# A hybrid encoder layer: the second copies of the dilated heads' high halves are loaded, and w_out's low parts are made on GpSimd in two steps

## The chip, the cores and the metric

One core of one Trainium2 chip runs the kernel. The time is the device time of one execution in microseconds (us). Engines are named as in the profile: PE is TensorE's matmuls, DVE is VectorE, ACT is ScalarE, POOL is GpSimd, SP is SyncE, which here issues the DMAs.

## The reference

```python
h = layer_norm(x, g_emb, b_emb)                     # (1, 2048, 1024)
proj = h @ w_in                                     # a_q a_k a_v a_g c_q c_kv b_kr b_g m_q m_g
y_a = dilated_attention(rope(a_q), rope(a_k), a_v)  # 16 heads of 64; (window, dilation) = (128,1), (512,4), (2048,16),
                                                    # each 64 neighbours a side; the three merged by their softmax sums
q = rms_norm(c_q) @ w_uq;  kv = rms_norm(c_kv) @ w_ukv
y_b = softmax((q_nope k_nope + q_rope k_rope) * 96**-0.5) @ v   # latent attention (MLA): 8 heads, all 2048 keys
y_m = softmax(m_q mk * 128**-0.5) @ mv                          # 4 heads on 256 memory tokens
y = concat(rms_norm(y_g) * silu(gate_g) for g in (a, b, m))     # (1, 2048, 2048)
out = layer_norm(alpha * h + y @ w_out, g_post, b_post)
```

All of it is float32. The kernel gets near that with 16-bit matmuls by splitting a number in a high part (its 16-bit rounding) and a low part (what the rounding left out): a product then takes three matmuls, high x high, high x low and low x high.

## The kernel before, in words

The work runs in four stages on the one core: layer norm, projections, gates and memory attention (0 to some 1370 us of the trace); the sixteen dilated heads (to 1745); the eight latent heads (to 2442); and the output stage, which transposes y and multiplies it by w_out (to the end). Instructions of an engine run in the order in which they were written; a wait of one holds all that stand behind it on its engine.

**A dilated head** is ten units: four of the first pattern, four of the second (u = 4 to 7), two of the third. A unit computes 128 x 1024 scores in PSUM (L1819 adds a mask, L1828 multiplies keys by queries), `probabilities` makes `pf` = exp(scores) on ACT (L1500), `ph`, its 16-bit rounding (on DVE, L1507 or L1513, or on ACT, L1505 or L1511), and `pl` = pf - ph (L1508 or L1514, on DVE or POOL); in the units 0 and 4 to 7 one half of `pf` goes through two selects on POOL (L1769) instead of a mask. `engines` (L1773) holds the choice: `pl` is on POOL in the units 1, 5, 6 and 8. `attend` multiplies by the values (L1521 to L1523), and `Out.add` copies a filled PSUM tile to the stage tile `so` (L1800, on DVE for the patterns 1 and 2). `Pipeline.push` writes a unit's multiplication by values three units behind its scores.

The scores of a head take two products over 128 and 65 rows: keys `ks` with queries `qs` (high parts in rows 0 to 63, low parts in 64 to 127), and `kk` with `q1`, which hold the other pairings: rows 0 to 63 of `kk` are the high keys again, rows 0 to 63 of `q1` are the lower half of `qs`. All of these tiles are named hq in the profile. `load_head` (L1289) loads `ks`, `qs` and a row of `q1` for the next head, into the other of two sets of tiles, when a head's first unit is written; SP issues it. `repeat_parts` (L1297) then makes the repeated rows, in four pieces of 512 columns each, the last of `kk` 768: of `kk` on ACT (L1302), of `q1` on DVE (L1304). `PIECES` (L1752) writes two of these copies behind each of the units 4 to 7 of the head before. For head 0 all eight stand at the end of the first stage.

**A latent head** is 4 blocks of 512 queries (n) by 8 units (k2) of 256 keys; a chunk below is one n of one head. Units are written in pairs by `push_two`. A unit multiplies keys by queries (L1654 to L1656), and two products of the running maximum of a later head stand beside it (L1602, into the PSUM tile `ps_x`), each reduced by DVE (`lmc`, L1608; `lmx`, L1612, ends sixteen of them). `pf`, `ph` and `pl` are as above; `lo_eng` (L1723) puts every third `pl` on POOL, the others on DVE. L1679 to L1681 multiply by the values; at a chunk's end L1686 and L1687 divide.

**w_out's 16 chunks of 128 rows** are scaled by a column `fw` and split in `woh` and `wol` in the latent heads 0 to 4 and the second chunk of head 5, one for each n of 1 to 3. In latent_units (L1696 to L1703) `load_raw` loads a chunk into the one float32 tile `wo_raw` at k2 = 0, `high` (L1988, ACT) makes `woh` at k2 = 4 and `low` (L1993, DVE) makes `wol` = raw x fw - woh at k2 = 6. At that k2 `busy` is set to 2: the next two `pl` go to POOL, and the count of three starts anew.

**The output stage** prepares its first tiles beside the last latent heads: `two` (L2032, POOL) and `three` (L2036, DVE) add the three patterns' results, `scale_a` and `scale_b` (L2045, L2048, POOL) multiply by gates.

Of the kernel before, what the change touches and what calls it, by code (L numbers as in the profile page):

```python
# [16 lines left out]
ALU = mybir.AluOpType  # L17
# [5 lines left out]
NT, NCH, NQ = S // P, D // P, S // 512  # L23
AH, AE = 16, 64
BH = 8
# [10 lines left out]
WRAP = 256  # L36
# [26 lines left out]
def tile_layer(ctx: ExitStack, tc: tile.TileContext, x, mem, pos, invf, sgn, g_embT, b_embT, g_emb, b_emb, w_in,  # L63
               g_cqT, g_ckvT, w_uq, w_ukv, w_mkv, g_outT, w_out, g_post, b_post, out):
    nc = tc.nc
# [34 lines left out]
    q_r = scratch("q_r", [AH, 2 * AE, S], F16)  # L100
    k_n = scratch("k_n", [AH, 2 * AE, S + WRAP], F16)
# [217 lines left out]
    sets, msets, vsets = [None, None], [None, None], [None, None]  # L319
    with ExitStack() as p1:  # L320
# [969 lines left out]
        def load_head(h):  # L1290
            ks, qs, q1, kk = sets[h % 2]
            nc.sync.dma_start(out=ks, in_=k_n[h])
            nc.sync.dma_start(out=qs, in_=q_r[h])
            nc.sync.dma_start(out=q1[64:65, :].rearrange("p (r k j) -> p r k j", r=16, k=8),
                              in_=AP(mneg, h * S, [[0, 1], [16, 16], [256, 8], [1, 16]]))

        def repeat_parts(h, i):  # L1297

            ks, qs, q1, kk = sets[h % 2]
            c = slice(512 * (i % 4), 512 * (i % 4) + 512 + (WRAP if i == 3 else 0))  # L1300
            if i < 4:
                nc.scalar.copy(kk[0:64, c], ks[0:64, c])  # L1302
            else:
                nc.vector.tensor_copy(q1[0:64, c], qs[64:128, c])  # L1304


        with tc.tile_pool(name="up", bufs=2, side="right", reuse_waits="tile") as up:
            gains = up.tile([P, 3], F32, bufs=1, name="gains")
# [175 lines left out]
        for n in (3, 0, 1, 2):  # L1484
            for g, w in zip((14, 15), two):
                gate_chunk(g, w, n, step)
            if n == 3:
                hpools[3].close()
                vs0 = early.enter_context(ExitStack())
                vsets[0] = value_set(vs0.enter_context(tc.tile_pool(name="vs0", bufs=1, side="right", reuse_waits="tile")))  # L1490
                vals0 = load_values(0)
                ones_rows(sets[0])
                for i in range(8):
                    repeat_parts(0, i)

    W2 = 1024
    def probabilities(pool, ps, scale, lo_engine, hi_engine=None, bufs=(4, 6), pair=None, select=None, bias=shift_t):
# [131 lines left out]
    def latent_units(h):  # L1629
# [62 lines left out]
        for n in range(NQ):  # L1692
            for k2 in range(8):
                if (n, k2) == (0, 0 if h else 2):
                    begin()
                if n and len(wol) < NT:  # L1696
                    if k2 == 0:
                        raws.append(load_raw(la, len(woh), 1))
                    if k2 == 4:
                        high(raws[0])  # L1700
                    busy[0] = 2 * (k2 == 6) or busy[0]
                    if k2 == 6:
                        low(raws.pop())  # L1703
                yield unit(n, k2)

    def all_heads():
# [11 lines left out]
                            ended.append((heads[h], m))  # L1718
                        yield

    lo_turn, busy = [0], [0]

    def lo_eng():  # L1723
        lo_turn[0] += 1
        if busy[0]:
            busy[0] -= 1
            lo_turn[0] = 0
            return nc.gpsimd
        return nc.gpsimd if lo_turn[0] % 3 == 0 else nc.vector

    raws, planned = [], {}
    ended = []
# [16 lines left out]
    for g, i in ((2, 0), (1, 1), (0, 1), (1, 0), (0, 0)):  # L1749
        stage[g][i] = da.tile([P, 16, 130], F32, bufs=1, name=f"so{g}_{i}")  # L1750

    LO, HI, PIECES = (1, 5, 6, 8), (0, 2, 3, 4, 8), {4: (0, 4), 5: (1, 5), 6: (2, 6), 7: (3, 7)}  # L1752


    BARE = {4: (1,), 5: (1,), 6: (1,), 7: (1,), 0: (1,)}
# [154 lines left out]
    def all_units():  # L1910
        vals = vals0
        for h in range(AH):
            if h % 2 and h + 1 < AH:
                following = load_values(h // 2 + 1)
            units = head_units(h // 2, h % 2, vals)
            if h == 0:
                ones_rows(sets[1])
            if h + 1 < AH:
                load_head(h + 1)
                for i, unit in enumerate(units):  # L1920
                    yield unit
                    for piece in PIECES.get(i, ()):
                        repeat_parts(h + 1, piece)
                    if h + 2 == AH and i == 4:
                        vs0.close()
                if h + 2 == AH:
                    s0.close()
            else:
                lvp = late.enter_context(tc.tile_pool(name="lv", bufs=1, side="right", reuse_waits="tile"))
                lv.extend(lvp.tile([P, NT * 258], F16, name=f"lv{i}") for i in range(2))  # L1930
                msets[0] = head_set(m0.enter_context(tc.tile_pool(name="m0", bufs=1, side="right", reuse_waits="tile")), 0, F16)
                head = Head(0)
                load_lv(0)
                for i, unit in enumerate(units):
                    yield unit
                    if i in MAXU:
                        max_tile(head, MAXU.index(i))
                    if i == 8:
                        head.max_turn(0, bank("s"))
            if h % 2 and h + 1 < AH:  # L1940
                vals = following
# [25 lines left out]
    with ExitStack() as p4:  # L1967
# [7 lines left out]
        woh = []  # L1975
# [9 lines left out]
        def high(raw):  # L1985
            c = len(woh)
            woh.append(wo0.tile([P, D], F16, name=f"woh{c}"))
            nc.scalar.activation(woh[c], raw, AF.Copy, scale=fw[:, c:c + 1])  # L1988

        def low(raw):  # L1990
            c = len(wol)
            wol.append(wo0.tile([P, D], F16, name=f"wol{c}"))
            nc.vector.scalar_tensor_tensor(out=wol[c], in0=raw, scalar=fw[:, c:c + 1], in1=woh[c], op0=ALU.mult, op1=ALU.subtract)  # L1993

        y_of, gates = {}, {}

# [315 lines left out]
```

## Time and profile before

| what | value |
|---|---|
| median of 3 runs | 2823.1 us (2821.95, 2823.10, 2834.79) |
| profiled execution | 2826.99 us, span 2825.1 us |
| latent stage, 1745 to 2442 us: PE / DVE / ACT / POOL busy | 661 / 560 / 558 / 270 us of 697 |
| dilated stage, 1370 to 1745 us: PE / DVE / ACT / POOL busy | 331 / 317 / 320 / 307 us of 375 |
| data moved | 347 MB, mean 123 GB/s |

A row of a group reads: line, engine, operation, tiles out<-in, shapes and count, then busy time in us and the mean of one in ns, then the idle time of the engine just before these instructions and what ended most of it. A row of the timeline has the start (us from the span's start), the duration, and in brackets the idle time before it. A row of the view of waits: us in total, times, longest.

### The profile page before, as it was taken

What the parts mean: (1) busy time and instruction counts of PE and PEld (TensorE: products, weight loads), DVE (VectorE), ACT (ScalarE), POOL (GpSimd) and SP (SyncE); (2) the same over time, 40 slices, a digit from 0 to 9 for tenths busy, and PEclk for the clock granted to TensorE, in tenths of its full rate; (3) what the DMA queues carried; (4) which work ended last, traced back from release to release, by engine and by line L of the source; (5) the groups of instructions that cost most, each with busy time, mean ns of one, the idle gap of its engine ahead of it and who ended that gap; (6) DMA issues with size and microseconds to landing.
All of it is one profiled execution on the core that took longest, in us unless ns stands there. A gap on an engine that the chain in (4) does not pass through costs nothing.

```text
span 2825.1 us, 56944 instructions
## 1 busy us (share of the span) xinstructions
PE 2666.0 (94%) x22765; PEld 1604.6 (57%) x22765; DVE 1926.0 (68%) x4427; ACT 1612.3 (57%) x2197; POOL 970.1 (34%) x649
## 2 busy tenths in 40 slices
PE   7989999999999999989988888999999999899998
PEld 6644445545546675455677776555555656545444
DVE  7524244449994576744588879788777878577776
ACT  6645434442123565544688887788777868533332
POOL 5301013342233000211588885434444333222221
PEclk9999999999999999999999999999999999999999
DMA  5556336682224212467488785212212030256663
GB/s 168 153 170 188 94 104 164 166 194 88 82 87 149 72 42 75 131 198 211 157 183 202 215 158 119 58 31 67 62 50 59 17 78 12 74 173 187 187 190 102
DMA packets 280489, 347.32 MB, mean 123 GB/s; under 512 B 38816, under 2 KB 209056, under 8 KB 279200
## 3 DMA queue, kind: packets, MB, share of 16 engines
q1 hardware_dynamic: 280224, 343.69, 44.0%
q8 instruction: 178, 2.92, 0.4%
q14 instruction: 87, 0.71, 0.1%
HBM read 216.13 MB, written 127.45 MB: 122 GB/s over the span
## 4 chain that ended last, share of the span: by engine, by line
PE 45%; DVE 9%; issue 4%; DMA 4%; ACT 3%; POOL 2%; SPq 0%; DVEq 0%; ACTq 0%; POOLq 0%
PE ps_s L2115 10%; PE ps_mm L189 6%; PE ps_x L1602 3%; PE ps_s L1654 3%; PE ps_s L1655 3%; PE ps_s L1656 3%; PE ps_o L1680 2%; PE ps_o L1681 2%; PE ps_o L1679 2%; PE ps_x L189 2%; PE ps_s L1828 2%; DVE lmc L1608 2%; PE ps_x L2115 1%; ACT pf L1500 1%; DVE pl L1514 1%
## 5 line engine op out<-in xcount | busy, mean ns | idle before, releaser
L189 PE MATMUL ps_mm<-hT,w_h 128*128 128x512 f16 x2880 | 862.9, 382 | 6.1 <-DVE rp L669 3.1
L189 PE MATMUL ps_mm<-hT,w_l 128*128 128x512 f16 x1440 | 547.3, 381 | 0.2 <-DVE w_l L396 0.2
L1514 POOL TENSOR_TENSOR pl<-pf,ph 128x1024 f16<-128x1024 f32 x134 | 342.1, 2556 | 450.1 <-ACT ph L1511 368.0
L189 PEld LDWEIGHTS <-w_h 128*128 128x128 f16 x2880 | 271.6, 99 | 277.5 <-issue 25.4
L1608 DVE TENSOR_REDUCE lmc<-ps_x 128x1 f32<-128x512 f32 x496 | 318.3, 684 | 123.8 <-PE ps_x L1602 122.8
L1500 ACT ACTIVATE pf<-ps_s,lscale 128x1024 f32<-128x1024 f32 x256 | 285.9, 1117 | 126.2 <-PE ps_s L1656 108.9
L1511 ACT ACTIVATE ph<-ps_s,lscale 128x1024 f16<-128x1024 f32 x254 | 283.9, 1118 | 0.0
L1514 DVE TENSOR_TENSOR pl<-pf,ph 128x1024 f16<-128x1024 f32 x200 | 270.8, 1355 | 4.7 <-ACT ph L1511 1.9
L189 PEld LDWEIGHTS <-w_l 128*128 128x128 f16 x1440 | 141.4, 98 | 172.2 <-issue 3.1
L1681 PE MATMUL ps_o<-lv,pl 128*128 128x65 f16 x2032 | 211.5, 197 | 7.4 <-POOL pl L1514 7.4
L1679 PE MATMUL ps_o<-lv,ph 128*128 128x65 f16 x2032 | 212.3, 197 | 0.0
L1680 PE MATMUL ps_o<-lv,ph 128*128 128x64 f16 x2032 | 211.9, 199 | 0.0
L1500 ACT ACTIVATE pf<-ps_s,shift_t,ascale 128x1024 f32<-128x1024 f32 x160 | 191.2, 1209 | 32.3 <-PE ps_s L1828 16.7
L1679 PEld LDWEIGHTS <-ph 128*128 128x128 f16 x2032 | 194.5, 99 | 22.1 <-issue 10.7
L1654 PE MATMUL ps_s<-hq,hq 97*128 97x512 f16 x512 | 198.0, 387 | 6.7 <-ACT ph L1511 3.4
L1680 PEld LDWEIGHTS <-ph 128*128 128x128 f16 x2032 | 194.8, 100 | 16.0 <-issue 2.0
L1681 PEld LDWEIGHTS <-pl 128*128 128x128 f16 x2032 | 194.4, 102 | 7.7 <-POOL pl L1514 7.6
L1655 PE MATMUL ps_s<-hq,hq 96*128 96x512 f16 x512 | 197.2, 385 | 0.0
L1656 PE MATMUL ps_s<-hq,hq 96*128 96x512 f16 x512 | 195.4, 382 | 0.0
L966 DVE CUSTOM_DVE_ANT_0 d1j<-ps_x,wm 128x256 bf16<-128x256 f32 (+1 forms) x608 | 184.5, 364 | 2.2 <-PE ps_x L963 1.4
L1828 PE MATMUL ps_s<-hq,hq 128*128 128x256 f16 (+3 forms) x1536 | 185.2, 259 | 0.0
L1602 PE MATMUL ps_x<-hq,hq 96*128 96x512 f16 x496 | 154.7, 384 | 30.8 <-DVE lmc L1608 30.7
(416 smaller groups left out, 5874.0 us busy)
## 6 DMA issues: line engine op xcount, KB each, us to landing
w_raw<-in_w_in_dram SPq DMA_DIRECT2D x56, 512.0 KB
oa<-oa_d SPq DMA_DIRECT2D x48, 520.0 KB
v<-va_d SPq DMA_DIRECT2D x24, 1032.0 KB
oa_d<-so SPq DMA_DIRECT2D x16, 1040.0 KB
gate_d<-sg SPq DMA_DIRECT2D x64, 256.0 KB
lv<-gate_d SPq DMA_DIRECT2D x15, 1024.0 KB
hq<-k_n SPq DMA_DIRECT2D x16, 576.0 KB
oa_d<-so SPq DMA_DIRECT2D x32, 260.0 KB
```

The costliest lines, as they stand in the source:

```text
L189: nc.tensor.matmul(ps, R(a), R(b), start=(i == 0), stop=(i == n - 1))
L1500: nc.scalar.activation(pf, ps, AF.Exp, bias=bias, scale=scale)
L1511: nc.scalar.activation(ph, ps, AF.Exp, bias=bias, scale=scale)
L1514: pipe.later.append(lambda: lo_engine.tensor_tensor(out=pl, in0=pf, in1=ph, op=ALU.subtract))
L1608: nc.vector.tensor_reduce(out=self.mc[:, t % 4, n:n + 1], in_=ps, axis=AX.X, op=ALU.max)
L1654: nc.tensor.matmul(b, R(cur.kh[0:97, kc]), R(cur.qh[0:97, c]), start=True, stop=False)
L1655: nc.tensor.matmul(b, R(cur.kh[0:96, kc]), R(cur.ql[0:96, c]), start=False, stop=False)
L1656: nc.tensor.matmul(b, R(cur.kl[0:96, kc]), R(cur.qh[0:96, c]), start=False, stop=True)
L1679: nc.tensor.matmul(o, ph, v[:, 0:65], start=(k2 == 0 and j == 0 and i == 0), stop=False, skip_group_check=True)
L1680: nc.tensor.matmul(o[:, 0:64], ph, v[:, 65:129], start=False, stop=False, skip_group_check=True)
L1681: nc.tensor.matmul(o, pl, v[:, 0:65], start=False, stop=(k2 == 7 and j == 1 and i == 3), skip_group_check=True)
L2115: nc.tensor.matmul(po[a // 512][:, a % 512:a % 512 + b - a], R(y[:, kc]), R(w[:, a:b]), start=(k == 0 and i == 0), stop=(k == NT - 1 and i ...
```

## The change

1. `load_head` issues two more DMAs on SP for each head, from DRAM, for the repeated rows of `kk` and `q1`; `repeat_parts`, `PIECES` and the eight copies of head 0 are gone.
2. `low` is two instructions on POOL: `scaled` at k2 = 5 multiplies `wo_raw` by `fw` in place, and `low` at k2 = 7 subtracts `woh`. `high` moves from k2 = 4 to 3.
3. `lo_eng` counts every third `pl` to POOL throughout, without `busy`; in the last chunk (`tail`: head 7, n = 3) all `pl` are on DVE.

```diff
         def load_head(h):
             ks, qs, q1, kk = sets[h % 2]
             nc.sync.dma_start(out=ks, in_=k_n[h])
             nc.sync.dma_start(out=qs, in_=q_r[h])
+            nc.sync.dma_start(out=kk[0:64, :], in_=k_n[h][0:64, :])
+            nc.sync.dma_start(out=q1[0:64, :], in_=q_r[h][64:128, :])
...
-        def repeat_parts(h, i):
-            ks, qs, q1, kk = sets[h % 2]
-            c = slice(512 * (i % 4), 512 * (i % 4) + 512 + (WRAP if i == 3 else 0))
-            if i < 4:
-                nc.scalar.copy(kk[0:64, c], ks[0:64, c])
-            else:
-                nc.vector.tensor_copy(q1[0:64, c], qs[64:128, c])
...
-                for i in range(8):
-                    repeat_parts(0, i)
...
-                    if k2 == 4:
+                    if k2 == 3:
                         high(raws[0])
-                    busy[0] = 2 * (k2 == 6) or busy[0]
-                    if k2 == 6:
+                    if k2 == 5:
+                        scaled(raws[0])
+                    if k2 == 7:
                         low(raws.pop())
+                tail[0] = h == BH - 1 and n == NQ - 1
                 yield unit(n, k2)
...
     def lo_eng():
         lo_turn[0] += 1
-        if busy[0]:
-            busy[0] -= 1
-            lo_turn[0] = 0
-            return nc.gpsimd
-        return nc.gpsimd if lo_turn[0] % 3 == 0 else nc.vector
+        return nc.gpsimd if lo_turn[0] % 3 == 0 and not tail[0] else nc.vector
...
-                    for piece in PIECES.get(i, ()):
-                        repeat_parts(h + 1, piece)
...
+        def scaled(raw):
+            nc.gpsimd.tensor_scalar(out=raw, in0=raw, scalar1=fw[:, len(wol):len(wol) + 1], scalar2=None, op0=ALU.mult)
+
         def low(raw):
             c = len(wol)
             wol.append(wo0.tile([P, D], F16, name=f"wol{c}"))
-            nc.vector.scalar_tensor_tensor(out=wol[c], in0=raw, scalar=fw[:, c:c + 1], in1=woh[c], op0=ALU.mult, op1=ALU.subtract)
+            nc.gpsimd.tensor_tensor(out=wol[c], in0=raw, in1=woh[c], op=ALU.subtract)
```

The order of DVE's instructions in the second half of a dilated head, before (so_1_14624 and so_1_14623 are the stage tiles of the second and the first pattern's next turn, hq the tiles of keys and queries):

```order
L1800 COPY so_1_14624<-ps_o 128x6x65
L1304 COPY hq_14609<-hq_14608 64x512
L1507 CAST ph<-pf 128x1024
L1508 TENSOR_TENSOR pl<-pf,ph 128x1024
L1304 COPY hq_14609<-hq_14608 64x512
L1800 COPY so_1_14624<-ps_o 128x6x65
L1800 COPY so_1_14624<-ps_o 128x4x65
L1304 COPY hq_14609<-hq_14608 64x512 x2
L1800 COPY so_1_14623<-ps_o 128x6x65
```

And after, at the same place (the lines of the file are eleven less or so, the tiles' numbers others):

```order
L1789 COPY so_1_14618<-ps_o 128x6x65
L1498 CAST ph<-pf 128x1024
L1499 TENSOR_TENSOR pl<-pf,ph 128x1024
L1789 COPY so_1_14618<-ps_o 128x6x65
L1789 COPY so_1_14618<-ps_o 128x4x65
L1789 COPY so_1_14617<-ps_o 128x6x65
```

The four copies are gone from between the `so` copies, the cast and `pl`; nothing else has moved there.

DVE in the first latent chunks with a low part, before:

```order
L1608 TENSOR_REDUCE lmc<-ps_x 128x1 x4
L1612 TENSOR_REDUCE lmx<-lmc 128x4
L1514 TENSOR_TENSOR pl<-pf,ph 128x1024
L1993 SCALAR_TENSOR_TENSOR wol_22783<-wo_raw,fw,woh_22693 128x1024
L1608 TENSOR_REDUCE lmc<-ps_x 128x1 x2
```

There POOL has nothing but its `pl` (one row of them, x14, up to the first memset of the next head). After, POOL's order from the dilated heads' last two `pl` through the three chunks of head 0:

```order
L1505 TENSOR_TENSOR pl<-pf,ph 128x1024 x4
L1978 TENSOR_SCALAR wo_raw<-wo_raw,fw 128x1024
L1505 TENSOR_TENSOR pl<-pf,ph 128x1024
L1983 TENSOR_TENSOR wol_22688<-wo_raw,woh_22505 128x1024
L1505 TENSOR_TENSOR pl<-pf,ph 128x1024 x2
L1978 TENSOR_SCALAR wo_raw<-wo_raw,fw 128x1024
L1505 TENSOR_TENSOR pl<-pf,ph 128x1024
L1983 TENSOR_TENSOR wol_23053<-wo_raw,woh_22870 128x1024
L1505 TENSOR_TENSOR pl<-pf,ph 128x1024 x2
L1978 TENSOR_SCALAR wo_raw<-wo_raw,fw 128x1024
L1983 TENSOR_TENSOR wol_23418<-wo_raw,woh_23235 128x1024
L1505 TENSOR_TENSOR pl<-pf,ph 128x1024
```

The low part has left DVE's order, and POOL's has two more instructions for each chunk, at another place against the `pl` in each of the three: with `pl` at k2 = 0, 3, 6 one `pl` stands between the two, with 1, 4, 7 one as well, and with 2, 5 none.

More of the change, by code (lines that the diff above doesn't have):

```diff
@@ L1719, in maxima_ahead @@
                         yield
-    lo_turn, busy = [0], [0]
+    lo_turn, tail = [0], [False]
     def lo_eng():
         lo_turn[0] += 1
-        if busy[0]:
-            busy[0] -= 1
-            lo_turn[0] = 0
-            return nc.gpsimd
-        return nc.gpsimd if lo_turn[0] % 3 == 0 else nc.vector
+        return nc.gpsimd if lo_turn[0] % 3 == 0 and not tail[0] else nc.vector
     raws, planned = [], {}
@@ L1750, in tile_layer @@
         stage[g][i] = da.tile([P, 16, 130], F32, bufs=1, name=f"so{g}_{i}")
-    LO, HI, PIECES = (1, 5, 6, 8), (0, 2, 3, 4, 8), {4: (0, 4), 5: (1, 5), 6: (2, 6), 7: (3, 7)}
+    LO, HI = (1, 5, 6, 8), (0, 2, 3, 4, 8)
     BARE = {4: (1,), 5: (1,), 6: (1,), 7: (1,), 0: (1,)}
```

## The prediction

> **What bounds the kernel now.** The page's first part comes first: PE is busy for 94% of the span, so a change to the other engines is worth only what it takes from PE's waits or from its clock.
>
> ```profile
> PE 2666.0 (94%) x22765; PEld 1604.6 (57%) x22765; DVE 1926.0 (68%) x4427; ACT 1612.3 (57%) x2197; POOL 970.1 (34%) x649
> ```
>
> Next comes the view of waits in the two stages that the change touches, of which I show the rows on PE: first the dilated heads (1375 to 1740 us), then the latent heads (1760 to 2400 us).
>
> ```profile
> PE ps_o L1521 <- DVE so L1800: 30.0, 31, 2.1
> PE ps_o L1523 <- POOL pl L1508: 4.6, 11, 0.4
> ```
>
> ```profile
> PE ps_x L1602 <- DVE lmc L1608: 26.6, 21, 2.1
> ```
>
> So PE waits some 35 us for the dilated stage's DVE and POOL, and some 27 us for the running-maximum reductions of the latent stage. Nothing in the change can give more than these, plus what the clock loses behind them. A measurement of this kernel tells about 0.5% (14 us) from no change.
>
> **Edit 1: the duplicated halves are loaded, not copied.** The copies, from the groups by form:
>
> ```profile
> L1302 ACT COPY hq<-hq 64x512 f16<-64x512 f16 x48 | 28.9, 606 | 4.0 <-DMA hq<-k_n 4.0
> L1304 DVE COPY hq<-hq 64x512 f16<-64x512 f16 x64 | 44.0, 709 | 5.1 <-DMA hq<-mneg 3.4 <-DMA hq<-q_r 0.8
> ```
>
> VectorE loses 44.0 us of copies. What of it PE sees is read from the timeline of one steady head; a fence for each of DVE, POOL, ACT and PE follows (start, duration, operation, and in brackets the idle time before it).
>
> ```profile
> 1585.11 0.34 DVE L1304 COPY hq<-hq 64x512 f16<-64x512 f16 x1
> 1585.49 0.82 DVE L1507 CAST ph<-pf 128x1024 f16<-128x1024 f32 x1
> 1586.34 1.23 DVE L1508 TENSOR_TENSOR pl<-pf,ph 128x1024 f16<-128x1024 f32 x1
> 1587.59 0.42 DVE L1304 COPY hq<-hq 64x512 f16<-64x512 f16 x1
> 1587.94 0.88 DVE L1800 COPY so<-ps_o 128x390 f32<-128x390 f32 x2
> 1588.74 2.28 DVE L1304 COPY hq<-hq 64x512 f16<-64x512 f16 x2
> ```
>
> ```profile
> 1586.45 1.86 POOL L1769 TENSOR_SCALAR_AFFINE_SELECT pf<-pf 128x256 f32<-128x256 f32 x2 [0.70 <-ACT pf L1500]
> 1588.29 2.14 POOL L1508 TENSOR_TENSOR pl<-pf,ph 128x1024 f16<-128x1024 f32 x1
> 1590.38 0.95 POOL L1769 TENSOR_SCALAR_AFFINE_SELECT pf<-pf 128x256 f32<-128x256 f32 x2
> 1591.30 2.15 POOL L1508 TENSOR_TENSOR pl<-pf,ph 128x1024 f16<-128x1024 f32 x1
> ```
>
> ```profile
> 1584.46 0.61 ACT L1302 COPY hq<-hq 64x512 f16<-64x512 f16 x1
> 1585.18 1.21 ACT L1500 ACTIVATE pf<-ps_s,shift_t,ascale 128x1024 f32<-128x1024 f32 x1
> ```
>
> ```profile
> 1588.53 0.19 PE L1521 MATMUL ps_o<-v,ph 128*128 128x65 f16 x1 [1.41 <-DVE so L1800]
> 1593.50 0.20 PE L1523 MATMUL ps_o<-v,pl 128*128 128x65 f16 x1 [0.42 <-POOL pl L1508]
> ```
>
> The first PE wait (1.41) ends when `so` has emptied its PSUM tile, and two copies stand ahead of that `so` on DVE (0.34 and 0.42). Without them it could come some 0.76 earlier. But POOL's chain, two selects and `pl`, twice over, runs back to back from 1586.45 to 1593.45 and ends PE's second wait, so PE can gain over a head only what POOL's chain comes earlier. That chain is held at its start: two selects take 1.86 together where the next two take 0.95, because VectorE's `pl` (1586.34) runs beside the first one, and that `pl` stands behind the one copy of 0.34. So it comes earlier by 0.34 and the gap beside it, 0.38 us a head, and fifteen heads have such copies: 15 x 0.38 = **-5.7 us**. At one head a copy also waited 0.84 us for its load and the so-wait behind it was 2.15 instead of 1.41; I take **-1 us** for it. The bounds are 0, if the select meets VectorE's `pl` in the same way earlier on, and the whole 35 us of the two rows of waits. ACT's copies I cost at nothing: the next `pf` at 1585.18 starts as soon as its scores are there, 0.1 us after the copy has ended. If they were not covered, they would be worth at most 0.6 a piece.
>
> What is added are two DMAs a head on SP's queue (64 x 4608 bytes and 64 x 4096 bytes, 0.56 MB), for all heads 8.9 MB. The stage moves 194 GB/s at a DMA share of 0.82:
>
> ```profile
> 1500.00:1600.00 100.00, 90.17 (x1558) 79.24 (x1557) 84.92 (x91) 89.08 (x98) 85.84 (x71) 0.99 0.82 194
> ```
>
> A head takes 22.5 us, so the addition is 25 GB/s, or 13%. At the same rate the share goes to about 0.93, and there is room. The copies read what the loads brought in the middle of the head before; now the tiles are wanted only by the next head's scores. Cost taken: 0; the other end is a rival.
>
> **Edit 2: w_out's low parts go to POOL.** Before, one DVE instruction makes each of the 16. The answer for its line has the least, the median and the longest, the groups have the sum:
>
> ```profile
> L1993 DVE SCALAR_TENSOR_TENSOR wol<-wo_raw,fw,woh 128x1024 f16<-128x1024 f32 x16 | 39.2, 2448 | 0.0
> ```
>
> ```profile
> L1993 DVE SCALAR_TENSOR_TENSOR wol<-wo_raw,fw,woh x16: 1278/3148/3153, 1780.9 to 2219.7; 128x1024 f16<-128x1024 f32 x16
> ```
>
> With two lengths, 1.28 and 3.15, a sum of 39.2 is six short and ten long ones ((39.2 - 16 x 1.28) / 1.87 = 10.0). The rows around a long one, on DVE, POOL and PE:
>
> ```profile
> 1796.75 1.29 DVE L1608 TENSOR_REDUCE lmc<-ps_x 128x1 f32<-128x512 f32 x2 [0.79 <-PE ps_x L1602]
> 1797.95 1.22 DVE L1514 TENSOR_TENSOR pl<-pf,ph 128x1024 f16<-128x1024 f32 x1
> ...
> 1800.49 1.22 DVE L1514 TENSOR_TENSOR pl<-pf,ph 128x1024 f16<-128x1024 f32 x1
> 1801.62 3.15 DVE L1993 SCALAR_TENSOR_TENSOR wol<-wo_raw,fw,woh 128x1024 f16<-128x1024 f32 x1
> 1804.70 2.64 DVE L1608 TENSOR_REDUCE lmc<-ps_x 128x1 f32<-128x512 f32 x4
> ```
>
> ```profile
> 1800.90 7.94 POOL L1514 TENSOR_TENSOR pl<-pf,ph 128x1024 f16<-128x1024 f32 x3 [4.69 <-ACT ph L1511]
> ```
>
> ```profile
> 1795.03 0.38 PE L1654 MATMUL ps_s<-hq,hq 97*128 97x512 f16 x1
> 1799.98 0.38 PE L1654 MATMUL ps_s<-hq,hq 97*128 97x512 f16 x1
> 1805.43 0.59 PE L1602 MATMUL ps_x<-hq,hq 96*128 96x512 f16 x1 [2.14 <-DVE lmc L1608]
> ```
>
> The low part meets a `pl` on POOL and stands until that has let go of SBUF; the reductions stand behind it on DVE, and PE behind them. In the window right behind it (busy time of PE, PEld, DVE, ACT, POOL with counts, then granted clock, DMA share, GB/s) the clock falls to half:
>
> ```profile
> 1806.00:1807.00 1.00, 0.99 (x13) 0.70 (x12) 0.95 (x2) 0.00 (x0) 1.00 (x2) 0.50 0.76 258
> ```
>
> A pair of units takes 4.95 us (1795.03 to 1799.98) and a chunk four pairs, 19.8. The next low part came 23.79 us behind this one:
>
> ```profile
> 1825.41 3.15 DVE L1993 SCALAR_TENSOR_TENSOR wol<-wo_raw,fw,woh 128x1024 f16<-128x1024 f32 x1
> ```
>
> So a long one costs 4.0 us, of which the shown wait is 2.1 and the rest, 1.8, mostly clock; ten cost 40. That is what edit 2 removes.
>
> What it adds: on POOL a `scaled` and a `low` for each of 16 chunks. The nearest row to `scaled` is a multiplication by a column on POOL, on half as many elements; for `low` a `pl` on POOL that meets nobody:
>
> ```profile
> L826 POOL TENSOR_SCALAR sg<-sg,gf 128x512 f32<-128x512 f32 x36 | 56.7, 1574 | 169.6 <-ACT sg L824 163.8 <-PE ps_x L963 5.8
> 2447.22 2.12 POOL L1514 TENSOR_TENSOR pl<-pf,ph 128x1024 f16<-128x1024 f32 x1
> ```
>
> So `scaled` takes 2 x 1.57 = 3.1 and `low` 2.1. POOL has the time, but DVE's `pl` cannot run while POOL is in one of them, and they start as soon as POOL is free, wherever k2 puts them. I lay this out by hand for the chunks whose third `pl` falls on k2 = 2 and 5, from the start of the third pair (0). ACT's `ph` of k2 = 2 ends 3.8 us into the second pair:
>
> ```profile
> 1797.67 1.14 ACT L1511 ACTIVATE ph<-ps_s,lscale 128x1024 f16<-128x1024 f32 x1
> ```
>
> POOL's `pl` then ends at 1.0 (3.8 + 2.1 - 4.95) and `scaled` at 4.1. DVE reduces from 1.7 to 2.9 (1796.75 is 1.72 into its pair), then wants `pl` and gets it at 4.1 instead of 2.9. The next reductions start at 5.3, where PE needs them by about 5.1: stall 0.1. `low` runs from 5.35 to 7.5; DVE's next `pl`, wanted at 6.5, runs from 7.5 to 8.6, and the reductions that PE needs by 7.0 start then: stall 1.5. For the other two positions the same working gives 0.8 + 1.9 and 1.3 + 0.3. Six, five and five chunks: 6 x 1.6 + 5 x 2.7 + 5 x 1.6 = 31 us. Only the 1.9 is about as long as a stall that cost clock before: 5 x 1.8 = 9. Sum 40 against 40: edit 2 is a wash, **0**, between -35 (a stall of 0.3 in each chunk, the least of the above) and +20 (every chunk's stall costs clock). The raw tile's reload on SP now waits for POOL's `low` instead of DVE's, and ACT's `high` reads it a unit earlier; by the working above `low` ends in the chunk's fourth pair, before the next load is issued, so I cost it at 0. Were it late, SP's loads behind it and ACT's `pf` behind `high` would wait, and PE's scores behind those. The Trainium skill, SBUF — State Buffer, section "Who interferes with whom", speaks against this edit: a VectorE instruction with two SBUF inputs contends with a GpSimd one that reads SBUF, and the loser stands for the whole instruction. This trace agrees (3.15 against 1.28), so moving work to POOL does not free VectorE.
>
> **Edit 3: the last chunk's low parts on DVE.** PE's longest wait before the end:
>
> ```profile
> 2444.89 2.37 POOL L2032 TENSOR_TENSOR oa<-oa 128x1040 f32<-128x1040 f32 x1 [11.45 <-DMA oa<-oa_d]
> 2449.39 0.23 PE L1681 MATMUL ps_o<-lv,pl 128*128 128x65 f16 x1 [7.45 <-POOL pl L1514]
> 2450.50 1.24 DVE L2036 TENSOR_TENSOR oa<-oa 128x1040 f32<-128x1040 f32 x1 [13.64 <-POOL lv L2048]
> ```
>
> `pl` (2447.22) stands behind POOL's merge, which waits for a DMA; on DVE it doesn't. But the next `pl` stands on DVE behind the second merge (2450.50 to 2451.74), which waits for the load that the first lets go. PE's wait moves there: **-1 us** (0.5 to 2.5).
>
> Edit 3's other half (every third `pl`, without the reset) moves POOL's turns in the last three heads against the final stage's preparations; I cost it at 0, within 3 us.
>
> Sum: -5.7 - 1 + 0 - 1 = -7.7, from 2827.0 of the profiled execution to 2819.3; the median of the runs lies 3.9 lower, so **2815 us**, 0.3% faster: no change that a measurement can tell. Its own range is 2804 to 2832.
>
> **Rivals.**
> (B) POOL's steps leave VectorE alone or fall between its `pl`: the stalls go, and instead of 0 edit 2 gives -35: 2780 us. For: six of the sixteen found DVE and POOL apart (1.28). Against: the ten others. The Trainium skill, GPSIMD Engine Reference, § 4.1 "Engine selection", calls one-input work on GpSimd roughly line-rate, by which `scaled` would be about 1 us (an estimate) and this rival likelier; row L826 with 1.57 for half the elements differs, and it decides here. Chance 0.17.
> (C) The stalls of all 16 chunks cost clock. A wait of 2.1 did so before; from which length on it does is not shown, and it decides: if from 1.5, or if two short stalls of a chunk add up, all three positions pass it. 31 + 16 x 1.8 = 60 against 40 is +20, which makes 2835; where `scaled` also meets a second `pl` (0.5 more each), 2843. For: PE has no slack to make a stall good with. Against: the shortest stalls of my working are 0.1 to 0.8. Chance 0.18.
> (D) DMA becomes the dilated stage's bound: at 0.82 before, the loads come late for the next head, and each of 15 heads waits for 0.56 MB at 194 GB/s, 2.9 us: +43, 2858. Against: the loads are issued a head, 22.5 us, ahead of their use. Chance 0.05.
> (E) Edit 1 frees most of the 35 us, say 30, because POOL's chain shortens as well once no copy stands on DVE beside its selects: 2815 - 30 + 6.7 = 2792. For: the copies hold SBUF's port against POOL too. Against: POOL's two `pl`, 2.14 and 2.15, are as short as one that meets nobody (2.12). Chance 0.10.
> The change does what it says, as far as the order of instructions goes.
>
> **How the numbers follow.** My forecast has 0.50. Faster by over 0.5% (under 2809): B, E and an eighth of the first, 0.17 + 0.10 + 0.06 = 0.33. Slower (over 2837): D, half of C and the first's tail, 0.05 + 0.09 + 0.03 = 0.17. The rest, 0.50, is within. The range reaches into B and over most of C: 2783 to 2838.
>
> **What would show it.** Right: the view of waits still has PE waiting for `lmc` some 30 us, in more and shorter pieces; `wo_raw` TENSOR_SCALAR at 3.1 us; the so-wait of a dilated head near 1.0. Wrong: no waits for `lmc` in heads 0 to 4 (B); PE's clock below full in every chunk (C); PE waiting for `hq` DMAs (D); a head's period under 22.0 us (E).

## The result, and the profile after

The changed kernel takes 2778.1 us (median of 4 runs, 2776.8 to 2780.0) where the kernel before takes 2823.5: a ratio of 0.9828, with a 95% interval of 0.9814 to 0.9842. That is 45 us, or 1.7%, faster. The forecast was 2815, and the time lies below the low end of its range, 2783. Rival B had the size (2780); the forecast's own working of edit 2 failed. The two profiled executions lie 50 us apart (2827.0 and 2776.8), so the stages below add up to 50 and not to 45.

The engines' busy time after, from the page; PE has 95% of a shorter span:

```profile
PE 2641.6 (95%) x22718; PEld 1589.7 (57%) x22765; DVE 1875.7 (68%) x4367; ACT 1577.8 (57%) x2133; POOL 1003.6 (36%) x661
```

The trace says where the time went. The first latent scores start at 1736.5 us instead of 1741.4; the last latent product ends at 2409.5 instead of 2459.2; from there to the end it is 365.6 instead of 365.9. So the dilated stage gave 5 us, the latent one 45, the output stage nothing. In the latent stage the rows to compare are the wait of the maxima's product for its reductions (L1602 and L1608 before, now L1593 and L1599; 1760 to 2400 us)

```profile
PE ps_x L1593 <- DVE lmc L1599: 4.4, 5, 1.9
```

and the busy times and granted clock of heads 0 to 4, first before,

```profile
1760.00:2200.00 440.00, 416.80 (x5146) 253.05 (x5145) 353.54 (x486) 351.46 (x356) 185.66 (x76) 0.97 0.20 54
```

then after:

```profile
1760.00:2200.00 440.00, 439.50 (x5662) 267.56 (x5662) 375.56 (x537) 386.12 (x392) 237.45 (x95) 1.00 0.21 56
```

26.6 us of waits have become 4.4, of which 3.7 are two waits in the last heads. In 440 us PE is now idle for 0.5, and its clock is full where it was 0.97.

What POOL's two new steps do to VectorE, from the timeline of the first chunk with them, POOL and then DVE:

```profile
1768.57 2.85 POOL L1978 TENSOR_SCALAR wo_raw<-wo_raw,fw 128x1024 f32<-128x1024 f32 x1 [0.70 <-ACT woh L1975]
...
1775.11 2.13 POOL L1983 TENSOR_TENSOR wol<-wo_raw,woh 128x1024 f16<-128x1024 f32 x1
```

```profile
1769.62 1.22 DVE L1505 TENSOR_TENSOR pl<-pf,ph 128x1024 f16<-128x1024 f32 x1
...
1776.50 1.82 DVE L1505 TENSOR_TENSOR pl<-pf,ph 128x1024 f16<-128x1024 f32 x1
```

VectorE's `pl` at 1769.62 starts 1.05 us into `scaled` and runs through in its usual 1.22. So it goes in all sixteen chunks: in each, a `pl` starts 0.98 to 1.76 us after `scaled` and takes 1.21 or 1.22. Only `low` holds one up: the `pl` at 1776.50 by 0.6 us, and those of the other fifteen chunks by 0.1 to 0.6.

In the dilated stage the waits of PE, and two new rows (1375 to 1740 us):

```profile
PE ps_o L1512 <- DVE so L1789: 17.3, 31, 0.6
...
ACT so L1789 <- DMA oa_d<-so: 8.4, 2, 4.4
PE ps_o L1514 <- POOL pl L1499: 8.1, 14, 0.6
...
PE ps_o L1512 <- ACT so L1789: 3.2, 4, 1.0
```

and the three waits of a steady head:

```profile
1565.57 0.19 PE L1512 MATMUL ps_o<-v,ph 128*128 128x65 f16 x1 [0.62 <-DVE so L1789]
1570.85 0.20 PE L1514 MATMUL ps_o<-v,pl 128*128 128x65 f16 x1 [0.57 <-POOL pl L1499]
1575.95 0.19 PE L1512 MATMUL ps_o<-v,ph 128*128 128x65 f16 x1 [0.55 <-DVE so L1789]
```

The first wait went from 1.41 to 0.62, and POOL's rose from 0.42 to 0.57, as a chain that now binds does. A steady head takes 22.05 us instead of 22.53. But three heads of this execution take 24.5, 24.8 and 24.2 us. In the first two of them ACT waits 4 us until the stage tile's store (`oa_d<-so`) has let it go. Such a wait is in no profile of a kernel with the old copies, but odd heads, longer than the steady ones, are: by the same count (POOL's first copy of each head) the kernel before has heads of 24.0 and 25.9 us. From 1500 to 1600 us the DMA share is 0.95 at 218 GB/s, where the prediction had about 0.93.

### The profile page after: what moved, and what is told of

Same layout as the page of the kernel before. It is cut to its first block, busy times and chain, and to the rows that moved or that the text cites. A ratio compares the mean times of both kernels' runs of the same rounds, so it can differ in the third digit from the quotient of the medians.

```text
span 2775.1 us, 56812 instructions
## 1 busy us (share of the span) xinstructions
PE 2641.6 (95%) x22718; PEld 1589.7 (57%) x22765; DVE 1875.7 (68%) x4367; ACT 1577.8 (57%) x2133; POOL 1003.6 (36%) x661
## 4 chain that ended last, share of the span: by engine, by line
PE 41%; DVE 9%; DMA 6%; issue 4%; ACT 3%; POOL 3%; SPq 0%; DVEq 0%; ACTq 0%; POOLq 0%
PE ps_mm L189 6%; PE ps_s L2105 6%; PE ps_x L1593 3%; PE ps_s L1645 3%; PE ps_s L1646 3%; PE ps_s L1647 3%; PE ps_o L1671 2%; PE ps_o L1672 2%; PE ps_o L1670 2%; PE ps_s L1817 2%; PE ps_x L189 2%; DMA oa<-oa_d 2%; PE ps_x L2105 1%; DVE lmc L1599 1%; ACT pf L1491 1%
## 5 line engine op out<-in xcount | busy, mean ns | idle before, releaser
L1505 POOL TENSOR_TENSOR pl<-pf,ph 128x1024 f16<-128x1024 f32 x114 | 295.1, 2589 | 361.2 <-ACT ph L1502 339.8
L1599 DVE TENSOR_REDUCE lmc<-ps_x 128x1 f32<-128x512 f32 x496 | 318.3, 683 | 91.8 <-PE ps_x L1593 90.7
L1505 DVE TENSOR_TENSOR pl<-pf,ph 128x1024 f16<-128x1024 f32 x220 | 300.7, 1367 | 3.9 <-ACT ph L1502 2.7
L1672 PE MATMUL ps_o<-lv,pl 128*128 128x65 f16 x2032 | 201.6, 193 | 8.1 <-DVE pl L1505 8.1
L1670 PE MATMUL ps_o<-lv,ph 128*128 128x65 f16 x2032 | 202.3, 193 | 0.0
L1671 PE MATMUL ps_o<-lv,ph 128*128 128x64 f16 x2032 | 202.0, 195 | 0.0
L1670 PEld LDWEIGHTS <-ph 128*128 128x128 f16 x2032 | 188.9, 97 | 18.7 <-issue 6.0
L1671 PEld LDWEIGHTS <-ph 128*128 128x128 f16 x2032 | 188.9, 97 | 15.1 <-issue 0.3
L1672 PEld LDWEIGHTS <-pl 128*128 128x128 f16 x2032 | 188.6, 99 | 8.5 <-DVE pl L1505 8.4
L824 ACT ACTIVATE sg<-ps_mm,fun 128x512 f32<-128x512 f32 x64 | 44.0, 688 | 229.9 <-PE ps_mm L189 159.7
```

The source lines that it names most:

```text
L1505: pipe.later.append(lambda: lo_engine.tensor_tensor(out=pl, in0=pf, in1=ph, op=ALU.subtract))
L1599: nc.vector.tensor_reduce(out=self.mc[:, t % 4, n:n + 1], in_=ps, axis=AX.X, op=ALU.max)
L1670: nc.tensor.matmul(o, ph, v[:, 0:65], start=(k2 == 0 and j == 0 and i == 0), stop=False, skip_group_check=True)
L1671: nc.tensor.matmul(o[:, 0:64], ph, v[:, 65:129], start=False, stop=False, skip_group_check=True)
L1672: nc.tensor.matmul(o, pl, v[:, 0:65], start=False, stop=(k2 == 7 and j == 1 and i == 3), skip_group_check=True)
```

## The experiments

Times are medians beside runs of the kernel before on the same chip (2823 to 2825 us); the ratio is to these. Line numbers differ a little from kernel to kernel.

**One edit at a time.** Theory "free multiplication": `scaled` does not hold VectorE and `low` hardly does, so moving the low part off VectorE removes the stalls. Rival "reset": the stalls came from `busy`, which sent two `pl` to POOL at the place of the low part.

e1_loads, edit 1 alone: the kernel before with

```diff
+            nc.sync.dma_start(out=kk[0:64, :], in_=k_n[h][0:64, :])
+            nc.sync.dma_start(out=q1[0:64, :], in_=q_r[h][64:128, :])
...
-                        repeat_parts(h + 1, piece)
```

> Only the loads in place of the copies (edit 1); the latent stage as before. The changed kernel's first latent scores come 4.9 us earlier than before's. If that is all that edit 1 gives: 2818 us, a dilated head in 22.06 instead of 22.52 us, and the ten stalls of the latent stage still there. If the loads' freedom reached into the latent stage as well (rival: part of the 45 us comes from edit 1): under 2810.

Measured: 2817.0 us, ratio 0.9973 (0.9960 to 0.9986), heads of 22.05 us, the ten waits of 2.1 all there. Edit 1 gives 8 us alone (4 to 11) and does not reach into the latent stage.

e2_pool_low, edit 2 alone: the changed kernel with the old copies and

```diff
+                    busy[0] = 2 * (k2 == 6) or busy[0]
                     if k2 == 5:
                         scaled(raws[0])
...
-        return nc.gpsimd if lo_turn[0] % 3 == 0 and not tail[0] else nc.vector
+        if busy[0]:
+            busy[0] -= 1
+            lo_turn[0] = 0
+            return nc.gpsimd
+        return nc.gpsimd if lo_turn[0] % 3 == 0 else nc.vector
```

> Only the low parts on POOL in two steps (edit 2); copies as before, and the turns of pl as before, with the reset at k2 = 6. Theory 'free multiplication' (POOL's multiplication by a column does not hold VectorE's pl, and low holds it for little): the stalls go also with the reset, some 35 us, 2788 us (2780 to 2796). Theory 'reset' (the stalls came from sending two pl in a row to POOL at the place of the low part): they stay, 2813 to 2824. My prediction's working (both steps hold VectorE): about 2823.

Measured: 2782.8, ratio 0.9855 (0.9830 to 0.9881). The stalls go with the reset in place; the waits that are left are few:

```profile
PE ps_x L1603 <- DVE lmc L1609: 6.0, 6, 2.0
```

Edit 2 alone is worth 42 us. "Reset" as the only cause is out.

e3_every_third, edit 3 alone: the kernel before without the line with `busy` and with the new `lo_eng`.

> Only the plain every-third turns, and the last chunk's pl on VectorE (edit 3); the low part stays on VectorE in one step at k2 = 6. Theory 'free multiplication': the low part of two inputs still meets a pl on POOL in most chunks, and where it doesn't DVE has a pl more beside it: 2800 to 2825. Theory 'reset': the stalls are gone, 2783.

Measured: 2802.2, ratio 0.9921 (0.9893 to 0.9950). Half the gain (14 to 30 us) comes with the low part still on VectorE. The row of the low part says why:

```profile
L1989 DVE SCALAR_TENSOR_TENSOR wol<-wo_raw,fw,woh 128x1024 f16<-128x1024 f32 x16 | 34.1, 2128 | 0.0
```

34.1 us instead of 39.2: six of the sixteen take 3.15 now, and there are six waits of 2.1 instead of ten; five others take 1.75 and cost none.

e4_latent_both, edits 2 and 3: the changed kernel with `repeat_parts` and `PIECES` put back and the two loads taken out.

> The changed kernel with the old copies (edits 2 and 3 without edit 1). Both theories: 2783 us, the changed kernel's time and the 4.9 us that its latent stage starts earlier. If edit 1's extra DMA traffic hurts somewhere or helps in the latent stage, the difference to the changed kernel is another than 5 us.

Measured: 2779.0, ratio 0.9841 (0.9822 to 0.9860): in heads 0 to 4 edits 2 and 3 take away the same waits, so they don't add up there, and edit 1's 8 us are not seen on top of them (0.9828, the intervals overlap). In head 6, behind them, edit 3 does add something: it takes 86.8 us here and 93.3 in e2_pool_low (from ACT's first `pf` of a head to that of the next), and one of its two waits for `lmc` is gone. In all the profiles head 6 takes 86.2 to 90.4 us with the new turns and 92.3 to 93.5 with the old. The medians of these two runs, 2779.0 and 2782.8, have intervals that overlap.

**What holds VectorE.** The changed kernel, with one more step on POOL for each chunk.

e5_low_twice:

```diff
             nc.gpsimd.tensor_tensor(out=wol[c], in0=raw, in1=woh[c], op=ALU.subtract)
+            nc.gpsimd.tensor_tensor(out=wol[c], in0=raw, in1=woh[c], op=ALU.subtract)
```

> The changed kernel with POOL's low issued twice (2.1 us more on POOL for each of 16 chunks, two inputs, the same result). If POOL's two-input steps hold VectorE's pl: pl and the reductions come up to 2 us later in each chunk, the waits for lmc come back in part of the 16, 5 to 30 us more than the changed kernel. If POOL's steps cost nothing as long as POOL has time: within 3 us of it.

Measured: 2773.8, ratio 0.9828 (0.9810 to 0.9846), as the changed kernel. The second subtraction and VectorE did get in each other's way, it takes 2.99 us instead of 2.13, and all of VectorE's `pl` together 320 us instead of 301, 1.2 more a chunk; but PE's waits are small (heads 0 to 4, with the busy times of the same 440 us):

```profile
PE ps_x L1593 <- DVE lmc L1599: 1.7, 8, 0.2
```

```profile
1760.00:2200.00 440.00, 437.34 (x5594) 264.46 (x5593) 388.70 (x532) 382.31 (x387) 280.96 (x111) 1.00 0.20 55
```

So VectorE loses over a microsecond a chunk, in up to three holds of under 0.9 each, and PE is idle for 2.7 us of the 440 instead of 0.5. My expectation that such waits cost 5 to 30 us fell, but the step is not free: heads 0 to 4 take 407.7 us in this profile and 404.3 in that of the changed kernel. The whole time can't show these 3 us. It includes the dilated stage, which in this execution has no head over 23.1 us, so that the first latent scores come at 1729.5 instead of 1736.5.

e6_scaled_twice:

```diff
+        nc.gpsimd.memset(ones_fw, 1.0)
...
             nc.gpsimd.tensor_scalar(out=raw, in0=raw, scalar1=fw[:, len(wol):len(wol) + 1], scalar2=None, op0=ALU.mult)
+            nc.gpsimd.tensor_scalar(out=raw, in0=raw, scalar1=ones_fw, scalar2=None, op0=ALU.mult)
```

> The changed kernel with a second multiplication on POOL for each chunk (by a column of ones; 2.84 us more on POOL, one tensor input, the same result). If a multiplication by a column never holds VectorE, as the changed kernel's trace suggests: within 3 us of the changed kernel, or what low and pl lose by coming later. If it does (my prediction's working): 10 to 40 us more.

Measured: 2777.3, ratio 0.9840 (0.9818 to 0.9861): no change in the whole time either, again with a dilated stage without odd heads (none over 22.6 us). Heads 0 to 4 take 409.7 us, 5 more than in the changed kernel, and PE is idle for 5.0 of the 440:

```profile
1760.00:2200.00 440.00, 435.05 (x5556) 262.95 (x5553) 384.67 (x530) 380.96 (x386) 271.24 (x111) 1.00 0.20 55
```

The trace has a multiplication that does hold a `pl`, here the second one:

```profile
1886.68 2.84 POOL L1981 TENSOR_SCALAR wo_raw<-wo_raw,ones_fw 128x1024 f32<-128x1024 f32 x1
```

```profile
1887.05 1.82 DVE L1505 TENSOR_TENSOR pl<-pf,ph 128x1024 f16<-128x1024 f32 x1
```

The `pl` begins 0.37 us into it and takes 0.60 more than its 1.22: it is let in after 0.97. All `pl` of this run begun 0.37 to 0.45 us into a multiplication take 1.74 to 1.82, and all begun from 1.04 on take 1.21 or 1.22.

e7_beside, not the layer but operations beside each other:

```diff
+        def section(d, nd, g, ng):
+            ...
+            for _ in range(ng):
+                g()
+            for _ in range(nd):
+                d()
```

> Not the layer: sixteen short sections, each with twelve operations of one kind on VectorE beside four of one kind on POOL, on 128 x 1024 (and each alone); the output is one tile written sixteen times. If the number of tensor inputs decides: VectorE's two-input operations (the subtraction and the low part's old form) take their 1.2 us beside POOL's multiplication (2.84) and select, but wait beside POOL's subtraction. If any POOL operation that reads SBUF holds them: 3 us and more beside each of the three.

Alone, VectorE's subtraction takes 1.23 us and POOL's multiplication 2.84:

```profile
9.65 1.23 DVE L84 TENSOR_TENSOR pl<-pf,ph 128x1024 f16<-128x1024 f32 x1
```

```profile
44.68 2.84 POOL L96 TENSOR_SCALAR raw<-raw,col 128x1024 f32<-128x1024 f32 x1
```

Beside POOL's multiplication (one of 3.22 us), two of VectorE's subtractions pass in 3.28 us, the first held up by 0.8 (2.02 us), the second free:

```profile
73.37 3.22 POOL L96 TENSOR_SCALAR raw<-raw,col 128x1024 f32<-128x1024 f32 x1
```

```profile
73.92 3.28 DVE L84 TENSOR_TENSOR pl<-pf,ph 128x1024 f16<-128x1024 f32 x2
```

Beside POOL's subtraction only one passes for each of POOL's (two of these in 6.21 us), and takes 3.03:

```profile
84.95 6.21 POOL L99 TENSOR_TENSOR gl<-raw,gh 128x1024 f16<-128x1024 f32 x2 [5.04 <-DVE ph L111]
```

```profile
89.22 3.03 DVE L84 TENSOR_TENSOR pl<-pf,ph 128x1024 f16<-128x1024 f32 x1
```

The low part's old form on VectorE behaves the same (2.02 and 1.28 beside the multiplication, 3.02 beside the subtraction). POOL's select holds it too: beside it `pl` takes 1.53, and the select 1.50 instead of 0.63. So the multiplication does hold VectorE, against my expectation, and the select as well. For two-input operations it is the first part that counts: here a `pl` begun 0.55 us in was held for 0.8 (POOL itself had first stood behind the `pl` before, hence its 3.22), in e6_scaled_twice it was let in at 0.97, and in the changed kernel those begun from 0.98 on were not held. Of its 2.84 us about the first one counts. VectorE's 16-bit copy is held a second time, though: one begun 1.9 us into a multiplication takes 1.24 instead of 0.43. Why the copy is and `pl` is not, no run here shows.

e8_long_step, one step twice as long behind `low`, in place of the doubling:

```diff
+            nc.gpsimd.memset(y, 0.0)
...
+            nc.gpsimd.tensor_tensor(out=ys[0][0], in0=ys[0][0], in1=ys[0][1], op=ALU.subtract)
```

> The changed kernel with one longer two-input step behind each low on POOL: 128 x 2048 on tiles that are still unused (zeros, written later by what they are for), an estimated 4.2 us from the 2.12 of 128 x 1024. Doubling low, in two steps of 2.1 us, cost no time, since VectorE gets in between. If the length of one hold decides (VectorE can be held up for about 2 us a chunk, not for 3): pl comes up to 4 us late, waits for lmc of 2 us and half clock come back in part of the chunks, 15 to 50 us more than the changed kernel. If only VectorE's own instructions matter: within 5 us of it.

Measured: 2800.3, ratio 0.9918 (0.9901 to 0.9934), 22 us more than the changed kernel (heads 0 to 4 alone take 430.4 instead of 404.3). The step takes 5.04 us, and in 440 us there are five waits of 1.75 and five of 0.8, with a clock of 0.98:

```profile
L1986 POOL TENSOR_TENSOR yh<-yh,yl 128x2048 f16<-128x2048 f16 x16 | 80.7, 5042 | 0.0
```

```profile
PE ps_x L1593 <- DVE lmc L1599: 14.6, 18, 1.8
```

A second step of 2.1 costs heads 0 to 4 some 3 us and one of 5.0 in its place 26. These two runs differ in the sum of POOL's steps as well as in the length of one. What tells the two apart is this run's own trace, where the same step stands in all sixteen chunks and meets `pl` at three different places, of which the first and the last are:

```profile
1794.61 3.89 DVE L1505 TENSOR_TENSOR pl<-pf,ph 128x1024 f16<-128x1024 f32 x1
...
1817.65 2.58 DVE L1505 TENSOR_TENSOR pl<-pf,ph 128x1024 f16<-128x1024 f32 x1
```

In five chunks one `pl` is held for 2.7 us, and each has the wait of 1.75; in five for 2.4, and each has the wait of 0.8; in six for 1.4, and PE does not wait there. All holds of `pl` in a chunk together come to 2.8, 3.0 and 2.7. So it is the length of a single hold that goes with the wait, and not the sum: VectorE's waiting instruction gets in between two of POOL's. It is not the whole of it: in three chunks of e6_scaled_twice two holds of 0.5 and 0.6, on two `pl` with only reductions between them, made a wait of 0.7.

**What made the old stalls.** e9_low_apart, the kernel before with

```diff
             lo_turn[0] = 0
-            return nc.gpsimd
+            return nc.vector
```

> The kernel before, the low part still one instruction on VectorE, with one word changed: the two pl behind it go to VectorE instead of POOL, so that POOL is quiet beside the low part. If the meeting with a pl on POOL makes the stall: all sixteen low parts take 1.28, the ten stalls go, 2823 less 10 x 3.9 = 2785 (to 2795, since VectorE has up to 2.3 us more to do there). If VectorE's load makes it (rival): the stalls stay or grow, 2820 or more.

Measured: 2824.6, ratio 1.0003 (0.9993 to 1.0012). The expectation of 2785 fell, but not the mechanism: the low part still meets a `pl`, one that POOL had already begun.

```profile
1796.28 2.85 POOL L1514 TENSOR_TENSOR pl<-pf,ph 128x1024 f16<-128x1024 f32 x1 [4.63 <-ACT ph L1511]
```

```profile
1797.07 3.15 DVE L1993 SCALAR_TENSOR_TENSOR wol<-wo_raw,fw,woh 128x1024 f16<-128x1024 f32 x1
```

It is the `pl` of k2 = 5, which the reset does not move. What the run does show is that two more `pl` a chunk on VectorE cost nothing.

e12_quiet takes that `pl` away:

```diff
+                    quiet[0] = 2 * (k2 == 4) or quiet[0]
...
         lo_turn[0] += 1
+        if quiet[0]:
+            quiet[0] -= 1
+            return nc.vector
         if busy[0]:
```

> The kernel before, with the pl of the units k2 = 4 and 5 on VectorE in the chunks with a low part; the low part and the two pl behind it stay where they were (VectorE, POOL). Unlike in the run that moved the two later pl, POOL's own pl of k2 = 5, which runs when the low part starts, is gone. If the meeting makes the stall: all low parts take 1.28 and the ten waits of 2.1 are gone or under 1, 2823 - 35 to 2823 - 40: 2783 to 2795. If VectorE's load makes it: 2815 or more, with waits beside low parts of 1.28.

Measured: 2800.0, ratio 0.9918 (0.9903 to 0.9933). All sixteen low parts take 1.28, the waits of 2.1 are gone, and 23 us with them:

```profile
L1997 DVE SCALAR_TENSOR_TENSOR wol<-wo_raw,fw,woh x16: 1277/1279/1280, 1776.7 to 2192.6; 128x1024 f16<-128x1024 f32 x16
```

```profile
PE ps_x L1602 <- DVE lmc L1608: 10.6, 40, 0.3
```

So the meeting makes the long waits, and it is worth 23 us. The other 20 are not there: in the ten chunks PE now waits four times 0.2 to 0.3, because the low part's own 1.28 and the next `pl`, held up by the two that the reset sends to POOL in a row, stand on VectorE one behind the other:

```profile
1797.45 1.28 DVE L1997 SCALAR_TENSOR_TENSOR wol<-wo_raw,fw,woh 128x1024 f16<-128x1024 f32 x1
...
1799.84 2.98 DVE L1514 TENSOR_TENSOR pl<-pf,ph 128x1024 f16<-128x1024 f32 x1
```

Both theories have a part. Heads 0 to 4 take 442.5 us before, 418.7 here and 404.2 in e2_pool_low, whose turns in the last heads are the same as here; PE is idle for 10.6 us of the 440 here and for 0.7 there. So 10 of the 14.5 us between the two are waits; the other 4 or 5 I can't assign.

**The added loads.** e11_loads_twice, the changed kernel with each of the two added loads issued twice.

> The changed kernel with each of the two added loads issued twice (0.56 MB a head more, the same data). If the added traffic is hidden (my prediction's step): heads of 22.05 us as in the changed kernel, within 4 us of it. If it costs the heads something: as much again as it costs now, seen as PE waiting for loads or ACT waiting for its stage tile's store.

Measured: 2810.8, ratio 0.9956 (0.9941 to 0.9971), 33 us more. Most heads still take 22.05 us, but four take 30 or 31 and one 25.3. In the dilated stage ACT waits for its stage tile's store, and PE for ACT:

```profile
ACT so L1791 <- DMA oa_d<-so: 42.4, 5, 10.7
...
PE ps_o L1514 <- ACT so L1791: 27.4, 4, 7.4
```

What comes late is not the new loads but a store.

e13_kk_copied, the changed kernel with `kk` copied on ACT again:

```diff
-            nc.sync.dma_start(out=kk[0:64, :], in_=k_n[h][0:64, :])
...
+                    if 4 <= i < 8:
+                        repeat_parts(h + 1, i - 4)
```

> The changed kernel with the rows of kk copied on ACT again (as before) and only those of q1 loaded: half of the added bytes. If ACT's copies are hidden (my prediction's step): heads of 22.05 us stay, and the odd heads of 24 us of the changed kernel's profile go or shrink, 0 to 8 us less than the changed kernel. If they are not: heads of 22.1 to 22.5 us, 1 to 7 us more.

Measured: 2773.2, ratio 0.9825 (0.9807 to 0.9844). Steady heads keep 22.05 us with 42 us of copies back on ACT, so these are indeed hidden. The odd heads have not gone (25.1, 25.0 and 26.7 in this profile, whose execution took 2780.6 us where the other three took 2771.5 to 2774.7), and the difference to the changed kernel is within the intervals.

**A faster version.** PE's longest wait after the change is in the last chunk; PE, and what VectorE does just ahead of that `pl`:

```profile
2401.63 0.24 PE L1672 MATMUL ps_o<-lv,pl 128*128 128x65 f16 x1 [8.11 <-DVE pl L1505]
```

```profile
2399.19 1.24 DVE L2026 TENSOR_TENSOR oa<-oa 128x1040 f32<-128x1040 f32 x1 [10.85 <-DMA oa<-oa_d]
```

e10_three moves that addition for the first two tiles, and issues the second tile's loads and `two` earlier:

```diff
-                nc.vector.tensor_tensor(out=self.oa[:, 0], in0=self.oa[:, 0], in1=self.oa[:, 1], op=ALU.add)
+                (nc.gpsimd if self in preps[:2] else nc.vector).tensor_tensor(out=self.oa[:, 0], in0=self.oa[:, 0], in1=self.oa[:, 1], op=ALU.add)
...
-        for at, *fs in (((7, 3, 4), p.load, p.load_m, p.load_b, p.load_h), ((7, 3, 6), p.two), ((7, 3, 7), p.three)):
+        for at, *fs in (((7, 2, 6), p.load), ((7, 3, 3), p.two), ((7, 3, 4), p.load_m, p.load_b, p.load_h), ((7, 3, 7), p.three)):
```

> The changed kernel, with the third pattern's addition of the first two output tiles on POOL instead of VectorE, and the second tile's loads issued half a chunk earlier. PE waits 8.1 us for a pl that stands on VectorE behind that addition in the last chunk, and 1.9 us and clock in head 6 behind the other. Both should go; what the output stage's own chain doesn't take back is gain: 2 to 10 us less than the changed kernel.

Measured: 2755.2, ratio 0.9753 (0.9737 to 0.9769): some 21 us less than the changed kernel by the ratios, more than expected. The wait of 8.1 is gone, and of those in the last heads one of 1.8 is left:

```profile
PE ps_x L1593 <- DVE lmc L1599: 2.0, 2, 1.8
```

The latent stage is 14 us shorter from its first scores to its last product (658.6 for 673.1). The profiled execution took 2765.0 us, the other three 2752 to 2757, so where these gained the rest no trace shows.

e14_three_kk is e10_three with the `kk` copies of e13_kk_copied.

> The two that may beat the changed kernel together: the third pattern's addition on POOL for the first two output tiles with earlier loads (0.9753 of before), and kk copied on ACT. If traffic costs the changed kernel something in most executions: 2745 to 2755; if not, 2755 as without.

Measured: 2764.5, ratio 0.9791 (0.9775 to 0.9808), slower than without the copies; this run was on another chip, with the kernel before at 2822.8 there and 2823.6 beside e10_three. The expectation fell. Its profile has heads of 24.8 and 23.0 us, that of e10_three none over 22.5; which copies or loads make odd heads in which execution stays open.

## Why the prediction was wrong

**Edit 2** was forecast at 0 and is worth 42 us alone. Its first half, 4.0 us for each of ten long low parts, holds: removing them gave just that. What failed is the step "DVE's `pl` cannot run while POOL is in one of them". For `scaled` it can, from 0.97 us on, and in the sixteen chunks it always came later than that, the earliest at 0.98. That none came sooner is in part luck: in e5_low_twice and e6_scaled_twice some came 0.4 us in and were held for 0.5 to 0.6. `low` does hold it, as assumed, but with `scaled` out of the way the `pl` comes when `low` is at least two thirds done and is 0.6 us late at most, not 1.0 on top of an earlier delay. The durations were right (2.84 for 3.1, and 2.13 for 2.1).

A second assumption in the same working was too strict: that the reductions have no room beyond the few tenths that I gave them. In e8_long_step a `pl` held for 1.4 us cost PE no wait, and doubling `low` made VectorE's `pl` 1.2 us a chunk longer while PE waited at most 0.2 at a time. Only long single holds, the low part's 3.15 on VectorE or a `pl` held for 2.7 by POOL's step of 5.0, made waits of 1.75 to 2.1 with a drop of the clock behind them. So the 31 us of stalls and 9 of clock that I set against the 40 were 0.5 us of idle time and a full clock.

My evidence for the step was in the trace of before, but only from a two-input `pl` against the two-input low part, and I carried it over to a one-input operation. The rule on the shared pair that I cited (the Trainium skill, SBUF — State Buffer, "Who interferes with whom") has the loser stand for the whole instruction; beside POOL's subtraction the runs agree (3.03 for 1.23), beside its multiplication they differ (1.22 for 1.22, one microsecond in). The rule beside rival B, that one-input work on GpSimd is roughly line-rate (the Trainium skill, GPSIMD Engine Reference, § 4.1 "Engine selection"), did not come out either: `scaled` takes 2.84 us, more than the subtraction. Rival B was right in what happened, not through that rule.

**Edit 1** was forecast at -6.7 and measured -8 (alone). The chain was right: POOL's selects and `pl` bind after it, and a head gained 0.48 us where 0.38 was worked out. That ACT's copies cost nothing was right as well. That the loads cost nothing is shown for a steady head only. Three heads of the profile after lost 2 us or more each, about what the others gained, but this can't be put to the loads as a whole: the kernel before has such heads with its copies (24.0 and 25.9 us), and e1_loads, e5_low_twice, e6_scaled_twice, e8_long_step and e10_three have the same loads and no head over 23.1. What comes with the loads alone is ACT's wait for the store, 4.0 and 4.4 us in two of the three heads. The room was small: the same bytes again cost 33 us.

**Edit 3**: for the tail -1 was forecast; the wait moved from POOL's `pl` to VectorE's behind `three`, as the step said, and is 8.1 instead of 7.45, so the gain is none. Its other half, the turns without the reset, was costed at 0 within 3; alone it took 23 us, since it moves the third `pl` away from four of the ten meetings. With edit 2 in place these meetings are gone anyway, but by the profiles the turns still give 2 to 7 us in head 6, where the working had 3 at most.

## What to carry to other kernels

When an engine has to get out of another's way, count first how long a single instruction holds it, not how much time the holds take in sum: waiting work slips in between two short ones, unless they follow directly on each other. To price a small step, compare the stage in which it stands: here the dilated stage moved the whole time by more than a doubled step did. Measure the pair of operations that will really meet, since a subtraction and a multiplication on the same engine hold others very differently. And a wait taken away can be found again behind the next instruction in the queue: moving that one, the addition in the last chunk, and its loads brought a further 0.75%.

## What the hardware showed that was not expected

A multiplication by a column on GpSimd (128 x 1024, float32) takes 2.84 us, a subtraction of two tensors 2.12. The slower one holds VectorE's two-input subtraction only at its start (let in at 0.97 us in e6_scaled_twice); the faster one holds it to its end (in all sixteen chunks of the changed kernel `pl` ended 1.08 us after `low`, and 1.22 is its length alone).

VectorE's conversion to 16 bits and its 16-bit copy, with a single input from SBUF, wait for GpSimd as well: in e7_beside they took 2.49 and 2.22 us beside the subtraction, 0.69 and 0.43 alone. Beside the multiplication they took up to 1.49 and 1.24.
